# Gathering rows with repeated indices: the first index lists worked out in groups, and five direct batches instead of three

One core of one Trainium2 chip. The metric is the device time of one execution in us, the median of several; a profiled execution gives a trace beside it (its "span" is some 2 us shorter than the device time).

## The reference

```python
# x: (32, 512, 1024) float32, indices: (32, 128) int in 0..511, a fixed random draw
for b in range(32):
    result[b] = x[b, indices[b]]          # (128, 1024) float32
```

A batch writes 128 rows of 4096 B. Its 128 indices repeat: the draw has 109 to 120 distinct ones per batch.

## The kernel before

It reads a repeated row once. For a *direct* batch it gathers all 128 rows and stores them. For a *sparse* batch, VectorE and TensorE first make a list of the distinct indices (with places that spread them evenly over the partitions); GpSimd gathers these rows into one of eight ring buffers, with the unused places out of bounds and so skipped; a matmul with a 0/1 matrix `s` spreads them to the 128 output rows; ScalarE copies these out of PSUM and a store follows. The index work of a sparse batch, three steps in the order of the program (`# ...` and `...` mark cuts; the lines that allocate tiles are left out):

```python
HEAD, RING, FAR, AHEAD = 3, 8, 1024, 9        # HEAD direct batches
pe, dve = InOrder(tc), InOrder(tc)            # what goes through these keeps its program order
# ...
for b in range(HEAD):
    gather(blocks[b], first[...] if b == 0 else idxT[:, b:b + 1], b)
    store(b)
# ...
def step0(b):      # cnt: how many earlier places hold the same index
    pe(mm, bc[:], lhsT=ident[:, col(b)].to_broadcast([N, N]), rhs=vf[:], ...)
    dve(v.scalar_tensor_tensor, out=junk[:], in0=bc[:], scalar=idxF[:, col(b)], in1=below[:], ...,
        accum_out=cnt[:, col(b)])
    dve(... lead16 = (cnt == 0)); dve(... lead = (cnt == 0))
def step1(b):      # nth: which distinct index it is; slot: where it goes
    pe(mm, sm[:, 0:1], lhsT=above[:], rhs=lead16[:, col(b)], ...)
    dve(... nth = sm); dve(... nth ^= shift); dve(... slot = nth)
    dve(v.tensor_scalar, out=pack[:], in0=turn[:], scalar1=slot[:, col(b)], scalar2=lead[:, col(b)], ...)
def step2(b):      # at: the list for the gather; s: the spreading matrix
    pe(mm, sm[:, 0:1], lhsT=pack[:], rhs=near[:, col(b)], ...)
    dve(... at = sm + FAR); dve(... atF = sm + FAR)
    dve(v.tensor_scalar, out=s[:], in0=bc[:], scalar1=atF[:, col(b)], ...)
# ...
for t in range(HEAD, HEAD + AHEAD + 2):       # eleven rounds ahead of any spread
    steps(t)                                  # step0(t), step2(t - 2), step1(t - 1)
    if t - 2 < HEAD + RING:
        fetch(t - 2)                          # gather into a ring buffer
for b in range(HEAD, B):
    spread_rows(b)                            # matmuls ps, copies, store
    fetch(b + RING)
    steps(b + AHEAD + 2)
```

## Time and profile before

| | before |
|---|---|
| time, us | 92.3 (92.2 to 92.9) |
| span of the profiled run, us | 90.1 |
| moved by DMA, MB | 31.99 |
| DMA rate on the plateau, GB/s | 418 |
| sparse gathers ahead of the first spread | 8, one in 1.83 us |
| first spread (start; end of its four matmuls), us | 20.7; 24.4 |

The page cuts the span into 40 slices and gives for each what the DMA engines moved. The useful reading is the *loss*: for a slice of width w and rate r it is (1 - r/418) x w. Added to the bytes over 418 GB/s, the losses give the span; that is so by construction, since the slices together hold all the bytes. The prediction shows the lines themselves.

### The profile page before, as it was taken

The page shows a single profiled execution, that of the slowest core. Times are in us where ns is not written, and L with a number is a line of the kernel's source. Part 1 is how long each engine was busy: PE and PEld are TensorE (multiplying, and loading weights), DVE is VectorE, ACT ScalarE, POOL GpSimd, SP SyncE. Part 2 cuts the span into 40 slices and gives each one's busy share as a digit, 9 for nine tenths or more (in the row PEclk, how much of TensorE's full clock was granted, in tenths as well). Part 3 has the DMA queues.
Part 4 walks back from the last instruction along what each step waited for, and adds up shares of the span by engine and source line. Part 5 has one row for each costly group of instructions (what it writes and reads, how often), then busy time and mean ns, then how long its engine had stood idle before and what let it go on. Part 6 is the DMA issues. An engine that isn't in the chain of part 4 may idle for free.

```text
span 90.1 us, 1046 instructions
## 1 busy us (share of the span) xinstructions
PE 63.1 (70%) x204; PEld 25.6 (28%) x204; DVE 51.3 (57%) x329; ACT 42.9 (48%) x67; POOL 33.7 (37%) x46
## 2 busy tenths in 40 slices
PE   0123232228999999999999999999999988882000
PEld 0110010004434343433434343433444333330000
DVE  2689899988097979787887979797200000000000
ACT  6999300000465555656565655556676755443000
POOL 7764665453054545444444545454440000000000
PEclk9999999999999999999999999999999999999955
DMA  0089999999659999999999999999999999999960
GB/s 2 13 253 324 333 260 393 407 415 411 256 207 249 396 387 420 409 416 416 420 420 415 411 416 418 424 415 420 409 424 418 415 424 413 424 418 418 424 280 7
DMA packets 9415, 31.99 MB, mean 355 GB/s; under 512 B 1590, under 2 KB 1622, under 8 KB 9409
## 3 DMA queue, kind: packets, MB, share of 16 engines
q1 hardware_dynamic: 4800, 16.81, 46.2%
q0 software_dynamic: 4608, 15.12, 44.6%
q14 instruction: 6, 0.04, 0.1%
q8 instruction: 1, 0.02, 0.1%
HBM read 16.81 MB, written 16.78 MB: 373 GB/s over the span
## 4 chain that ended last, share of the span: by engine, by line
DVE 36%; PE 31%; DMA 17%; issue 4%; POOL 1%; ACT 1%; SPq 0%; POOLq 0%; DVEq 0%
PE ps L24 27%; DMA u<-in_x_dram,at 15%; DVE junk L24 7%; DVE s L24 7%; DVE pack L24 6%; DVE nth L24 5%; DVE lead L24 5%; DVE slot L24 3%; PE pos L24 2%; DMA vals<-in_indices_dram 2%; DVE atF L24 1%; DVE at L24 1%; POOL u L110 1%; PE rk L24 1%; ACT block L196 1%
## 5 line engine op out<-in xcount | busy, mean ns | idle before, releaser
L24 PE MATMUL ps<-u,s 128*128 128x512 f32 x116 | 57.1, 625 | 1.5 <-DMA u<-in_x_dram,at 1.5
L196 ACT COPY block<-ps 128x512 f32<-128x512 f32 x58 | 34.0, 586 | 38.5 <-PE ps L24 38.0
L110 POOL DMA_INDIRECT u<-in_x_dram,at x29 | 28.9, 997 | 31.4 <-PE rk L24 13.4
L24 PEld LDWEIGHTS ps<-u,s 128*128 128x128 f32 x116 | 20.5, 194 | 21.2 <-issue 13.2
L24 DVE SCALAR_TENSOR_TENSOR junk<-bc,idxF,below 128x128 f16<-128x128 f32 x29 | 10.1, 349 | 4.5 <-PE rk L24 4.5
L24 PE MATMUL bc<-vf,ident 128*128 128x128 f16 x29 | 6.8, 241 | 6.5 <-DVE s L24 6.5
L24 DVE TENSOR_SCALAR s<-bc,atF 128x128 f32<-128x128 f32 x29 | 10.2, 351 | 1.0
L24 PEld LDWEIGHTS <-pack 128*128 128x128 f16 x29 | 2.9, 100 | 25.1 <-DVE pack L24 24.4
L24 DVE TENSOR_SCALAR pack<-turn,slot,lead 128x128 f16<-128x128 f16 x29 | 9.1, 315 | 1.1
L24 PE MATMUL pos<-near,pack 128*128 128x1 f16 x29 | 5.2, 178 | 6.4 <-DVE pack L24 5.4
L188 ACT COPY u<-zero 128x1024 f32<-128x1024 f32 x8 | 7.7, 1040 | 0.0
L24 DVE TENSOR_SCALAR lead<-cnt 128x1 f16<-128x1 f32 (+1 forms) x58 | 6.2, 150 | 1.0
L24 PE MATMUL rk<-lead,above 128*128 128x1 f16 x29 | 4.8, 164 | 0.8 <-DVE lead L24 0.8
L24 DVE TENSOR_TENSOR nth<-nth,shift 128x1 int32<-128x1 int32 x29 | 4.6, 159 | 1.1
L24 DVE CAST slot<-nth 128x1 f32<-128x1 int32 x29 | 4.5, 154 | 1.0
L24 DVE TENSOR_SCALAR at<-pos 128x1 int32<-128x1 f32 x29 | 4.3, 149 | 0.8 <-PE pos L24 0.5
L24 PEld LDWEIGHTS <-ident 128*128 128x128 f16 x29 | 2.9, 103 | 5.6 <-issue 5.6
L24 DVE TENSOR_SCALAR atF<-pos 128x1 f32<-128x1 f32 x29 | 4.3, 149 | 0.0
L24 DVE CAST nth<-rk 128x1 int32<-128x1 f32 x29 | 4.3, 148 | 0.0
L24 PEld LDWEIGHTS <-above 128*128 128x128 f16 x29 | 3.1, 107 | 0.0
L21 PE MATMUL pos<-ident,vf 128*128 128x32 f16 x1 | 0.2, 209 | 3.2 <-DVE vf L24 3.2
L24 DVE DVE_READ_ACCUMULATOR junk<-bc,idxF,below 128x1 f32 x29 | 2.4, 83 | 0.0
(21 smaller groups left out, 8.3 us busy)
## 6 DMA issues: line engine op xcount, KB each, us to landing
out_dram<-block SPq DMA_DIRECT2D x32, 512.0 KB, 9.2
u<-in_x_dram,at POOLq DMA_INDIRECT x29, 8.9
vals<-in_indices_dram SPq DMA_DIRECT2D x1, 32.0 KB, 1.7
block<-in_x_dram,idxT POOLq DMA_INDIRECT x2, 6.1
first<-in_indices_dram SPq DMA_DIRECT2D x1, 1.0 KB, 1.8
block<-in_x_dram,first POOLq DMA_INDIRECT x1, 4.5
```

The source lines that it names most:

```text
L21: self.last = do(*args, **kw)
L24: self.last = do(*args, **kw)
L110: nc.gpsimd.indirect_dma_start(out=dst[:], out_offset=None, in_=xf[:], in_offset=bass.IndirectOffsetOnAxis(ap=at, axis=0), element_offset= ...
L188: nc.scalar.copy(out=u[:], in_=zero[:].to_broadcast([N, D]))
L196: nc.scalar.copy(out=blocks[b][:, w], in_=ps[:])
```

## The change

It wants the gathers out sooner and the first spread earlier. The first nine sparse batches are worked in groups of 2, 4 and 3: the narrow instructions (one column a batch) are done once for a group, and the scheduler may order the groups' instructions freely. Two more batches become direct, so that GpSimd has gathers to issue meanwhile. The rest of the batches go the old way. `...` marks cuts again, and lines that allocate tiles are left out.

```diff
-    HEAD, RING, FAR, AHEAD = 3, 8, 1024, 9
+    HEAD, RING, FAR = 5, 8, 1024
 ...
-        if not HEAD <= b < B:            # in step0, step1 and step2
+        if not grouped <= b < B:
 ...
+    def group(g0, g1):
+        n, w = g1 - g0, slice(g0, g1)
+        bc = pbc.tile([N, 4, N], F32, name="bc")
+        for b in range(g0, g1):
+            mm(bc[:, b - g0], ...)
+        for b in range(g0, g1):
+            v.scalar_tensor_tensor(out=junk[:], in0=bc[:, b - g0], ..., accum_out=cnt[:, col(b)])
+        for t in (lead16, lead):
+            v.tensor_scalar(out=t[:, w], in0=cnt[:, w], ...)
+        mm(rk[:, :n], lhsT=above[:], rhs=lead16[:, w], ...)
+        v.tensor_copy(out=nth[:, w], in_=rk[:, :n])
+        v.tensor_tensor(out=nth[:, w], in0=nth[:, w], in1=shift[:, w], op=ALU.bitwise_xor)
+        v.tensor_copy(out=slot[:, w], in_=nth[:, w])
+        for b in range(g0, g1):
+            v.tensor_scalar(out=pack[:], in0=turn[:], scalar1=slot[:, col(b)], scalar2=lead[:, col(b)], ...)
+            pe.last = mm(pos[:, b - g0:b - g0 + 1], lhsT=pack[:], rhs=near[:, col(b)], ...)
+        for t in (at, atF):
+            v.tensor_scalar(out=t[:, w], in0=pos[:, :n], ...)
+        for b in range(g0, g1):
+            dve.last = v.tensor_scalar(out=s[:], in0=bc[:, b - g0], scalar1=atF[:, col(b)], ...)
 ...
-    for t in range(HEAD, HEAD + AHEAD + 2):
-        steps(t)
-        if t - 2 < HEAD + RING:
-            fetch(t - 2)
+    bounds = (HEAD, HEAD + 2, HEAD + 6, HEAD + 9)
+    grouped = bounds[-1]
+    for g0, g1 in zip(bounds, bounds[1:]):
+        group(g0, g1)
+        for b in range(g0, g1):
+            if b < HEAD + RING:
+                fetch(b)
+    steps(grouped)
+    steps(grouped + 1)
     for b in range(HEAD, B):
         spread_rows(b)
         fetch(b + RING)
-        steps(b + AHEAD + 2)
+        steps(b + grouped - HEAD + 2)
```

More of the change, by code (lines that the diff above doesn't have):

```diff
@@ L133, in step0 @@
     def step0(b):
-        if not HEAD <= b < B:
+        if not grouped <= b < B:
             return
-        bcs[b] = bc = pbc.tile([N, N], F32, name="bc")
-        pe(mm, bc[:], lhsT=ident[:, col(b)].to_broadcast([N, N]), rhs=vf[:], start=True, stop=True)
+        bcs[b] = bc = pbc.tile([N, 4, N], F32, name="bc")[:, 0]
+        pe(mm, bc, lhsT=ident[:, col(b)].to_broadcast([N, N]), rhs=vf[:], start=True, stop=True)
         junk = junkp.tile([N, N], F16, name="junk")
-        dve(v.scalar_tensor_tensor, out=junk[:], in0=bc[:], scalar=idxF[:, col(b)], in1=below[:],
+        dve(v.scalar_tensor_tensor, out=junk[:], in0=bc, scalar=idxF[:, col(b)], in1=below[:],
             op0=ALU.is_equal, op1=ALU.mult, accum_out=cnt[:, col(b)])
@@ L147, in step1 @@
     def step1(b):
-        if not HEAD <= b < B:
+        if not grouped <= b < B:
             return
@@ L162, in step2 @@
     def step2(b):
-        if not HEAD <= b < B:
+        if not grouped <= b < B:
             return
@@ L172, in step2 @@
         spread[b] = s = pick.tile([N, N], F32, name=f"s{b}")
-        dve(v.tensor_scalar, out=s[:], in0=bcs[b][:], scalar1=atF[:, col(b)], scalar2=None,
+        dve(v.tensor_scalar, out=s[:], in0=bcs[b], scalar1=atF[:, col(b)], scalar2=None,
             op0=ALU.is_equal)
@@ L178, in fetch @@
             gather(held[(b - HEAD) % RING], at[:, col(b)], b, bounds_check=S - 1, oob_is_err=False)
+    def group(g0, g1):
+        n, w = g1 - g0, slice(g0, g1)
+        bc = pbc.tile([N, 4, N], F32, name="bc")
+        for b in range(g0, g1):
+            mm(bc[:, b - g0], lhsT=ident[:, col(b)].to_broadcast([N, N]), rhs=vf[:], start=True, stop=True)
+        for b in range(g0, g1):
+            junk = junkp.tile([N, N], F16, name="junk")
+            v.scalar_tensor_tensor(out=junk[:], in0=bc[:, b - g0], scalar=idxF[:, col(b)], in1=below[:],
+                                   op0=ALU.is_equal, op1=ALU.mult, accum_out=cnt[:, col(b)])
+        for t in (lead16, lead):
+            v.tensor_scalar(out=t[:, w], in0=cnt[:, w], scalar1=0.0, scalar2=None, op0=ALU.is_equal)
+        rk = psm.tile([N, B], F32, name="rk")
+        mm(rk[:, :n], lhsT=above[:], rhs=lead16[:, w], start=True, stop=True)
+        v.tensor_copy(out=nth[:, w], in_=rk[:, :n])
+        v.tensor_tensor(out=nth[:, w], in0=nth[:, w], in1=shift[:, w], op=ALU.bitwise_xor)
+        v.tensor_copy(out=slot[:, w], in_=nth[:, w])
+        pos = psm.tile([N, B], F32, name="pos")
+        for b in range(g0, g1):
+            pack = junkp.tile([N, N], F16, name="pack")
+            v.tensor_scalar(out=pack[:], in0=turn[:], scalar1=slot[:, col(b)],
+                            scalar2=lead[:, col(b)], op0=ALU.is_equal, op1=ALU.mult)
+            pe.last = mm(pos[:, b - g0:b - g0 + 1], lhsT=pack[:], rhs=near[:, col(b)], start=True, stop=True)
+        for t in (at, atF):
+            v.tensor_scalar(out=t[:, w], in0=pos[:, :n], scalar1=float(FAR), scalar2=None, op0=ALU.add)
+        for b in range(g0, g1):
+            spread[b] = s = pick.tile([N, N], F32, name=f"s{b}")
+            dve.last = v.tensor_scalar(out=s[:], in0=bc[:, b - g0], scalar1=atF[:, col(b)], scalar2=None,
+                                       op0=ALU.is_equal)
     def steps(t):
```

## The prediction

> **What bounds the kernel now.** I read the page's 40 slices first, because the kernel moves 32 MB and computes little. A slice is 90.1/40 = 2.25 us; the first line is the busy share of the DMA engines in tenths, the second what they moved.
>
> ```profile
> DMA  0089999999659999999999999999999999999960
> GB/s 2 13 253 324 333 260 393 407 415 411 256 207 249 396 387 420 409 416 416 420 420 415 411 416 418 424 415 420 409 424 418 415 424 413 424 418 418 424 280 7
> DMA packets 9415, 31.99 MB, mean 355 GB/s; under 512 B 1590, under 2 KB 1622, under 8 KB 9409
> ```
>
> From slice 16 to slice 38 the rate is flat, mean 418 GB/s. That plateau is the floor: 31.99 MB / 418 GB/s = 76.5 us. The span is 90.1, so 13.5 us were lost against the plateau, and a slice's loss is (1 - rate/418) x 2.25 us:
> - slices 1 to 3, before a stream exists: 2.24 + 2.18 + 0.89 = 5.3 us
> - slices 4 to 10 (324, 333, 260, then about 400): 2.05 us
> - slices 11 to 15, the hole (256, 207, 249, 396, 387): 3.2 us
> - the last two, emptying: 2.95 us
>
> So nothing done beside the plateau can matter, except its bytes; the hole and the slope ahead of it can. The table by stages says which engine is busy there (columns: stretch, its length, then busy us of each engine, TensorE clock, DMA share, GB/s):
>
> ```profile
> 0.00:7.00 7.00, 0.95 (x8) 0.53 (x8) 4.18 (x30) 6.25 (x7) 4.78 (x17) 1.00 0.32 94
> 7.00:22.00 15.00, 5.01 (x26) 2.00 (x26) 13.53 (x90) 2.69 (x3) 7.98 (x8) 1.00 1.00 364
> 22.00:29.00 7.00, 6.89 (x21) 2.66 (x20) 4.12 (x26) 3.30 (x6) 2.13 (x3) 1.00 0.73 243
> ```
>
> From 7 to 22 us VectorE (third busy figure) is 90% busy, and the transfers get eight gathers. Next the gathers themselves, in the timeline of GpSimd (start, duration):
>
> ```profile
> 5.43 0.94 POOL L110 DMA_INDIRECT block<-in_x_dram,idxT  x1 [0.30 <-issue]
> 7.26 1.00 POOL L110 DMA_INDIRECT u<-in_x_dram,at  x1 [0.89 <-DVE nth L24]
> 9.08 1.00 POOL L110 DMA_INDIRECT u<-in_x_dram,at  x1 [0.81 <-DVE nth L24]
> ...
> 20.04 1.00 POOL L110 DMA_INDIRECT u<-in_x_dram,at  x1 [0.83 <-DVE nth L24]
> 24.69 1.00 POOL L110 DMA_INDIRECT u<-in_x_dram,at  x1 [3.65 <-PE rk L24]
> ```
>
> Direct gathers (the first lines) come 1.25 us apart; sparse ones come every 1.83 us, held by VectorE's index work, and after the eighth there is none for 4.65 us. Why 1.83 is in VectorE's timeline, one period of it:
>
> ```profile
> 8.16 0.14 DVE L24 TENSOR_SCALAR at<-pos 128x1 int32<-128x1 f32 x1
> 8.22 0.15 DVE L24 TENSOR_SCALAR atF<-pos 128x1 f32<-128x1 f32 x1
> 8.40 0.35 DVE L24 TENSOR_SCALAR s<-bc,atF 128x128 f32<-128x128 f32 x1
> 8.67 0.15 DVE L24 CAST nth<-rk 128x1 int32<-128x1 f32 x1
> 8.85 0.16 DVE L24 TENSOR_TENSOR nth<-nth,shift 128x1 int32<-128x1 int32 x1
> 9.05 0.15 DVE L24 CAST slot<-nth 128x1 f32<-128x1 int32 x1
> 9.24 0.31 DVE L24 TENSOR_SCALAR pack<-turn,slot,lead 128x128 f16<-128x128 f16 x1
> 9.47 0.34 DVE L24 SCALAR_TENSOR_TENSOR junk<-bc,idxF,below 128x128 f16<-128x128 f32 x1
> ```
>
> Read the starts, not the durations: `at` to `atF` is 0.06 us, but an instruction that uses the result ahead of it comes 0.18 to 0.20 later (`nth`, `slot`, `pack`). Last, why the hole: in the order of the program eleven rounds of index work stand ahead of the first spread matmul on TensorE, and that one is also slow.
>
> ```profile
> 20.66 3.76 PE L24 MATMUL ps<-u,s 128*128 128x512 f32 x4
> 24.41 1.10 PE L24 MATMUL ps<-u,s 128*128 128x512 f32 x2
> ```
>
> Four of them take 3.76 us here and about 1.96 later. Until they end at 24.4 no ring buffer comes free and no new block can be stored: the three direct stores are done, the eight gathers drain, and the DMA engines stand empty.
>
> **What the Trainium skill says.** "DMA: Bandwidth & Descriptors", section "Where 436 GB/s comes from": the fabric allows 435 GB/s, but the HBM side, about 358, should bind. The trace agrees with the first and not the second: it holds 418 for 50 us, reads and writes of HBM together. I take 418. The same page, section "Queues, rings and completion order": each DMA engine takes turns between the queues that have work. I use this for reads and stores each getting half, some 209 GB/s; the page of before fits (median 8.9 us from issue to landing for a sparse gather, 9.2 for a store) but does not prove it. "VectorE: DVE Perf Modes", section "Two Vector instructions with no wait between them": a next instruction that is not held starts earlier, before the one ahead is finished. The trace agrees: 0.06 against 0.18 us. "SBUF — State Buffer", section "SBUF: two separate sides": VectorE in a two-port mode can lock GpSimd out while it writes a gather's descriptors. Here gathers take 0.94 to 1.00 us beside a 90% busy VectorE, so little of it shows; it is a rival below.
>
> **The change part by part.**
> 1. *Two more direct batches.* They read all 128 rows. The fixed draw has 115 and 111 distinct indices in batches 3 and 4, so 13 + 17 = 30 rows x 4096 B = 0.123 MB more, 0.29 us of plateau. In return, direct gathers need no index work: after those at 2.77, 4.18 and 5.43 two more follow at about 6.68 and 7.93. Five direct stores (2.6 MB) instead of three then wait on the store side.
> 2. *Grouped index work.* Ahead, a batch costs ten VectorE instructions and 1.83 us. In a group of n it costs four wide ones each (`junk` with its accumulator read some 0.34 from start to start, `pack` 0.23, `s` 0.27: 0.84 us) and seven narrow ones for all n. In free order the scheduler has put other groups' `junk` between dependent narrow ones, as the built program's order shows, so I count 0.13 us for a narrow one: 9 x 0.84 + 21 x 0.13 = 10.3 us, from 3.9 to about 14.5. Ahead it was eleven rounds to 20.2.
>    Is GpSimd ever kept waiting? The first group's `at` stands after five wide `junk` for three groups, two `pack` and small ones; summed with these distances it ends at about 7.8, later than the 6.48 of before. But then GpSimd is still at direct gathers until 8.9, so the first sparse one starts at about 9.2. The second group's `at` ends at about 10.7, the third's at about 13.4; gathers 1.3 us apart want them at 11.8 and 17. So all thirteen gathers go out 1.25 to 1.3 us apart, the last at about 18.5.
> 3. *The first spread comes earlier.* On TensorE only `bc` of two batches and one `rk` stand ahead of it now, ready at about 15. It then waits for its gather. At half the rate (209 GB/s from 7.3 us, with some 0.8 MB read before), five direct gathers and one sparse one, 3.09 MB, are there at about 18.3; the slow first four matmuls end at about 22, a little earlier than 24.4.
>    What fills the DMA engines until then? Stores until about 18.5 (2.6 MB at 209 from 7.3 is 12.5 us, held a little by landings), and from there reads alone: by 18.5 about 3.1 of 6.36 MB have been read, the other 3.2 MB last 7.7 us at 418, to 26. New stores come from about 22.5. No hole.
>
> The sum against before: the slope of 2.05 us gives back about 1.5 (slice 4 stays partly short), the hole of 3.2 about 3.0, the bytes cost 0.3: 4.2 us. Start and end stay. After, TensorE's loop of about 2.06 us a batch stays under the DMA's, (0.467 + 0.524 MB)/418 = 2.37 us, so VectorE and TensorE do not bind there. 92.3 - 4.2 = 88.1 us.
>
> **The rivals.**
> - *Reading ahead only moves the hole.* The ring still has eight buffers; if the first spread ended at 26 or later, it would run dry again. For it: the four slow matmuls, and the first group's `at` being later. Against: 3.5 us of margin above. It would give back 1 to 2 us: 89 to 90.
> - *VectorE's dense run slows GpSimd* to, say, 1.8 us a gather. Then the last goes out at 22; but five direct gathers give the reads a backlog that halves at 209 GB/s cannot use up by then, so it costs under 1 us: 88.5 to 89.
> - *The hole was only an idle queue that the later plateau makes up*, since the backlog of stores at the end (last gather landed at 79.5, stores on until 88) hides when things were read. That would make it no gain plus 0.3, 92.6. Against: bytes moved at a flat ceiling cannot be made up later; every us of an empty stretch lengthens the span.
> - *A better case*: slice 3 also fills, and the end shortens: 87.2.
>
> **Range and chances.** The floor argument leaves little room: 87.0 to 90.0 holds the first two rivals and the better case. 2% faster is 90.5; only the third rival, or a group order that stalls GpSimd, misses it. Faster 0.9, same 0.09, slower 0.01.
>
> **What would show each step.** Direct gathers 1.25 us apart up to 7.9 and sparse ones from about 9.2, at 1.3 us, none held by VectorE: step 1 and 2. The slices from 4 on at 390 or more and no slice under 380 up to the last two: step 3. First spread between 17 and 19.5 with its four matmuls near 3.8 us. Plateau still 418, 32.1 MB in all. I am wrong if a hole stands anywhere between 10 and 35 us, if the plateau itself changes, or if the sparse gathers stay near 1.8 us apart.

## The result, and the profile after

| | before | after |
|---|---|---|
| time, us (median; range) | 92.28; 92.20 to 92.94 | 89.27; 88.88 to 89.99 |
| ratio to before (95% interval) | | 0.967 (0.959 to 0.975) |
| span of the profiled run, us | 90.1 | 87.5 |

A ratio is the mean time of one kernel's runs over that of the other's runs of the same rounds, so it is not quite the ratio of the medians quoted beside it. Executions over 1.5% slower than the fastest of the same kernel are left out of the means. A median is that of all runs of a kernel; in fill_2mb, columns_head3, groups_head3_b and first_of_one it takes in one run that counts as slow, in the kernel before of the third group two.

It is 3.0 us faster (3.7 and 3.5 in two repeats below); 4.2 were forecast. First the slices of the changed kernel (2.19 us each), with the DMA engines' busy share above and GB/s below:

```profile
DMA  0088999999999999999999999999999999999960
GB/s 0 15 223 200 257 352 403 419 419 419 419 416 418 419 421 419 418 418 418 419 414 418 418 412 419 418 418 419 418 419 419 418 419 419 419 419 419 419 251 6
DMA packets 9413, 32.11 MB, mean 367 GB/s; under 512 B 1559, under 2 KB 1591, under 8 KB 9408
```

The plateau is 418 as before, 32.11 MB is what was forecast, and there is no hole: from slice 8 to slice 38 no slice is under 412. But slices 3 to 6 (223, 200, 257, 352) are no better than those of before. The "busy" of 0.8 to 0.9 above them is no sign of work: 200 GB/s are moved there. The table by stages, with the columns of the one in the prediction:

```profile
7.00:22.00 15.00, 3.32 (x16) 1.86 (x17) 7.54 (x47) 2.69 (x3) 9.87 (x10) 1.00 0.97 359
22.00:29.00 7.00, 6.89 (x23) 2.82 (x22) 4.99 (x34) 3.51 (x6) 2.66 (x3) 1.00 1.03 421
```

From 7 to 22 us VectorE's load is nearly halved (7.5 us for 13.5) and yet the transfers get 359 GB/s, for 364 before; from 22 to 29 us they get 421 for 243. That is the whole gain. The gathers of the changed kernel, in GpSimd's timeline (the first line is a direct one, the last is the first that reuses a ring buffer):

```profile
8.44 0.94 POOL L110 DMA_INDIRECT block<-in_x_dram,idxT  x1 [0.30 <-issue]
9.68 1.00 POOL L110 DMA_INDIRECT u<-in_x_dram,at  x1 [0.30 <-issue]
10.99 1.00 POOL L110 DMA_INDIRECT u<-in_x_dram,at  x1 [0.30 <-issue]
...
18.80 1.00 POOL L110 DMA_INDIRECT u<-in_x_dram,at  x1 [0.30 <-issue]
24.19 1.00 POOL L110 DMA_INDIRECT u<-in_x_dram,at  x1 [4.40 <-PE rk L24]
```

From the second (4.68) to the thirteenth the gathers go out 1.25 to 1.3 us apart and no sparse one waits for its index list. GpSimd still has nothing to issue for 4.4 us before 24.19, as before. The difference is that the engines still have work queued during this time: slices 10 to 13 (19.7 to 28.4 us) are at 416 to 419. The first spread on TensorE is hardly earlier:

```profile
20.44 3.48 PE L24 MATMUL ps<-u,s 128*128 128x512 f32 x4
23.87 1.96 PE L24 MATMUL ps<-u,s 128*128 128x512 f32 x4
```

And VectorE's timeline in one part of the groups shows what "once for a group" buys: wide instructions that don't need each other follow closely (four `pack` take 0.97 us together, one alone 0.31; four `s` take 1.13), and one narrow instruction serves three or four batches (128x3, 128x4).

```profile
9.15 0.97 DVE L200 TENSOR_SCALAR pack<-turn,slot,lead 128x128 f16<-128x128 f16 x4
10.05 0.15 DVE L194 CAST nth<-rk 128x3 int32<-128x3 f32 x1
10.41 0.16 DVE L204 TENSOR_SCALAR at<-pos 128x4 int32<-128x4 f32 x1 [0.21 <-PE pos L202]
10.49 0.15 DVE L204 TENSOR_SCALAR atF<-pos 128x4 f32<-128x4 f32 x1
10.56 0.15 DVE L195 TENSOR_TENSOR nth<-nth,shift 128x3 int32<-128x3 int32 x1
10.68 1.13 DVE L207 TENSOR_SCALAR s<-bc,atF 128x128 f32<-128x128 f32 x4
```

Where the time went, as losses against 418 GB/s, worked out from the slices of each profile (slices of before are 2.25 us, those of the others 2.15 to 2.24). "Floor" is the bytes over 418. Slices 18 to 38 lose 0.1 or less unless the text says so. The rows under the line are the experiments' profiles:

| kernel | floor | slices 1-3 | slices 4-9 | slices 10-17 | last two | span |
|---|---|---|---|---|---|---|
| before | 76.5 | 5.3 | 2.0 | 3.3 | 3.0 | 90.1 |
| after | 76.8 | 5.3 | 2.4 | 0.0 | 3.0 | 87.5 |
| — | | | | | | |
| again (the changed kernel) | 76.8 | 5.2 | 1.9 | 0.0 | 3.1 | 86.9 |
| after_b (the changed kernel) | 76.8 | 5.2 | 2.0 | 0.0 | 2.6 | 86.6 |
| head5_only | 76.8 | 5.2 | 2.1 | 0.9 | 2.7 | 87.7 |
| groups_head3 | 76.5 | 5.2 | 1.6 | 0.0 | 2.9 | 86.2 |
| groups_head3_b | 76.5 | 5.2 | 2.0 | 0.0 | 2.3 | 86.0 |
| groups_in_order | 76.5 | 5.3 | 2.2 | 0.6 | 2.6 | 87.2 |
| fill_2mb | 81.8 | 3.1 | 1.3 | 0.0 | 3.2 | 89.5 |

Two things stand out. The hole is worth 3.3 us, and every kernel of the table with groups in free order has none of it. The opening (slices 1 to 9) costs 6.8 to 7.7 us in all of them but fill_2mb (4.4), and the same kernel differs in it by 0.6 us from run to run (after 7.7, again 7.1).

### The profile page after: what moved, and what is told of

It reads as the page before. It is cut to its first block, busy times and chain, and to the rows that moved or that the text cites. A ratio compares the mean times of both kernels' runs of the same rounds, so it can differ in the third digit from the quotient of the medians.

```text
span 87.5 us, 931 instructions
## 1 busy us (share of the span) xinstructions
PE 58.3 (67%) x184; PEld 23.8 (27%) x184; DVE 41.8 (48%) x265; ACT 40.5 (46%) x63; POOL 33.6 (38%) x46
## 2 busy tenths in 40 slices
DMA packets 9413, 32.11 MB, mean 367 GB/s; under 512 B 1559, under 2 KB 1591, under 8 KB 9408
## 4 chain that ended last, share of the span: by engine, by line
PE 29%; DVE 29%; DMA 22%; issue 5%; another core or an unknown queue 4%; POOL 1%; ACT 1%; SPq 0%; POOLq 0%; DVEq 0%
PE ps L24 25%; DMA u<-in_x_dram,at 19%; DVE junk L24 5%; DVE s L24 3%; DVE pack L24 3%; DVE s L207 3%; DMA vals<-in_indices_dram 3%; DVE junk L188 3%; DVE lead L24 2%; DVE nth L24 2%; PE pos L24 2%; DVE slot L24 2%; DVE pack L200 1%; DVE atF L204 1%
## 5 line engine op out<-in xcount | busy, mean ns | idle before, releaser
L24 PE MATMUL ps<-u,s 128*128 128x512 f32 x108 | 53.9, 626 | 3.6 <-DMA u<-in_x_dram,at 3.6
L226 ACT COPY block<-ps 128x512 f32<-128x512 f32 x54 | 31.6, 585 | 39.4 <-PE ps L24 31.1
L110 POOL DMA_INDIRECT u<-in_x_dram,at x27 | 26.9, 997 | 26.2 <-PE rk L24 13.0
L24 PEld LDWEIGHTS ps<-u,s 128*128 128x128 f32 x108 | 18.8, 194 | 29.1 <-issue 16.0
L24 PE MATMUL rk<-lead,above 128*128 128x1 f16 x18 | 2.9, 163 | 5.2 <-DVE junk L24 5.2
L24 DVE TENSOR_SCALAR lead<-cnt 128x1 f16<-128x1 f32 (+1 forms) x36 | 3.9, 150 | 4.6 <-remote 4.1
L110 POOL DMA_INDIRECT block<-in_x_dram,idxT x4 | 3.8, 946 | 1.7 <-issue 0.9
L24 PE MATMUL bc<-vf,ident 128*128 128x128 f16 x18 | 3.9, 227 | 0.0
L24 DVE TENSOR_TENSOR nth<-nth,shift 128x1 int32<-128x1 int32 x18 | 2.9, 159 | 0.6
L24 DVE CAST slot<-nth 128x1 f32<-128x1 int32 x18 | 2.8, 154 | 0.6
```

The costliest lines, as they stand in the source:

```text
L24: self.last = do(*args, **kw)
L110: nc.gpsimd.indirect_dma_start(out=dst[:], out_offset=None, in_=xf[:], in_offset=bass.IndirectOffsetOnAxis(ap=at, axis=0), element_offset= ...
L226: nc.scalar.copy(out=blocks[b][:, w], in_=ps[:])
```

## The experiments

Theory: the span is bytes over 418 GB/s, plus what is lost while the DMA engines' queues are empty. The hole is the time between the queues running dry and the end of the first spread, which frees the first ring buffer and gives the first new store. What queues more work ahead of that moment, or brings it forward, closes the hole. (As worded this does not cover all of what came: see the opening under fill_2mb, and the dip of head5_only.) Rivals: only one of the two parts does it; it is the free order that does it. A second question was the opening, where the prediction missed: is it slow because queues are nearly empty, or because of what is read there?

Twelve runs were made in three groups, each group against the kernel before on the same chip (92.9, 92.3 and 92.7 us there). The second group (groups_head4, groups_in_order, fill_2mb, columns_head3) has no run of the changed kernel or of groups_head3 in it and was made on another chip than the other two, so there the ratios to before are what compares.

### again and after_b: the changed kernel twice more

No edit.

> The changed kernel itself, once more, as the control of this group. Expected 0.967 of before, about 89.3 us. Its profile tells what repeats: if VectorE's stretches of 2.0 and 1.7 us with no releaser (12 to 14 and 17 to 19 us of the profile after) are a property of the program they are there again at the same instructions; if they are chance they move. The opening slices (223, 200, 257 and 352 GB/s) should again be well under 418.

> The changed kernel again, as the control of this group. 0.960 to 0.967 of before so far; the loss against 418 GB/s after slice 9 should be zero again, and that of slices 1 to 9 between 7.1 and 7.7 us.

Measured: 89.23 us, ratio 0.960 (0.953 to 0.966), and 89.22 us, ratio 0.962 (0.957 to 0.967). No loss after slice 9. The opening is slow again; in again it reads 236, 260, 332, 371, 345 GB/s in slices 3 to 7.

VectorE's long stretches without a releaser repeat. "remote" in the brackets means that the profile found nothing on this core that ended the wait. In the profile after:

```profile
18.99 0.21 DVE L24 TENSOR_SCALAR lead<-cnt 128x1 f16<-128x1 f32 x2 [1.73 <-remote]
21.82 0.21 DVE L24 TENSOR_SCALAR lead<-cnt 128x1 f16<-128x1 f32 x2 [2.34 <-remote]
```

and in that of again:

```profile
18.45 0.22 DVE L24 TENSOR_SCALAR lead<-cnt 128x1 f16<-128x1 f32 x2 [1.73 <-remote]
21.24 0.21 DVE L24 TENSOR_SCALAR lead<-cnt 128x1 f16<-128x1 f32 x2 [2.31 <-remote]
```

The second stands at the same instruction with the same length in after_b and one_region too (2.32 and 2.35 us), so it belongs to the program and not to chance. The first does not: in these two runs it is 1.20 us, and ended by `junk`. Nor does the stretch of 2.0 us that the expectation named: in again the same `pack` waits 1.25 us, ended by `slot`. In groups_head3 neither of the two is there. What they are, I could not settle. A lock of GpSimd's against VectorE is not it, at least for the second: in again the last gather ahead of it ends at 19.37 and the next starts at 23.23. They cost no time here, since no slice after the ninth lost anything. The first spread of again starts at 19.2; in one_region below, where TensorE was ready by 17.9, it waited for its gather until 19.3.

### head5_only: the direct batches alone

```diff
 # on the kernel before
-    HEAD, RING, FAR, AHEAD = 3, 8, 1024, 9
+    HEAD, RING, FAR, AHEAD = 5, 8, 1024, 9
```

> The kernel before with HEAD 5 instead of 3 and nothing else: index work by single batches in program order. Theory A (the hole is closed by a backlog of reads, and two more direct batches make enough of it): sparse gathers go out from 9.7 us to about 20.6, reads last until about 28, the first spread ends near 25, so no hole: within 0.5 us of the changed kernel, about 89.3. Rival B (the grouped index work closes the hole, by letting the gathers out at 1.3 instead of 1.83 us and the spread start sooner): a hole of some 1.5 to 2.5 us stays, about 91 us.

Measured: 89.54 us, ratio 0.961 (0.954 to 0.968), beside 0.960 of the changed kernel in the same group. Its slices:

```profile
GB/s 0 15 241 295 286 319 375 420 418 418 420 418 417 398 394 321 392 402 413 417 417 420 405 418 417 418 418 418 417 418 420 420 422 418 420 418 422 420 316 13
```

Here the index work is all as before (the first spread starts at 22.8, two us *later* than before), and still the hole has shrunk from 3.3 to 0.9 us; what is left are the 394, 321 and 392 about 33 us. Theory A holds within its 0.5 us; it expected no hole, and a small one is there. A backlog of reads and stores does most of the work, without any faster index work. The dip that is left comes 6 us after the first spread ended (26.5), so it is not the gap that the theory words; neither are the smaller ones of groups_in_order and ring6 below, which also come after the first spread. What they come from was not tested.

### groups_head3 and groups_head3_b: the groups alone

```diff
 # on the changed kernel
-    HEAD, RING, FAR = 5, 8, 1024
+    HEAD, RING, FAR = 3, 8, 1024
```

> The changed kernel with HEAD 3 instead of 5: groups of 2, 4 and 3 in free order, three direct batches. Theory A (either part alone gives the DMA engines enough to do): eleven gathers 1.3 us apart, last at about 17, and the first spread at 15 to 20.5 us, ending 3.5 us later; queued reads and stores (6.9 MB) last to about 24: hole of at most 1 us, less by 0.3 us for the rows saved: 89 to 90 us. Rival B2 (the five direct batches close the hole, the groups do nothing): 91.5 to 92.3, as before.

> Three direct batches with groups in free order, again, beside the changed kernel with more rounds. If it is truly the better one, it is 0.3 to 0.8 us under after_b: 0.29 us for 30 rows that aren't read, the rest from an opening that loses less (6.8 against 7.1 to 7.7 us). If the two are the same, the difference of the first group of runs (0.955 and 0.960) was scatter.

Measured: 88.56 us, ratio 0.955 (0.947 to 0.962), and 88.99 us, ratio 0.960 (0.955 to 0.966). The slices of groups_head3:

```profile
GB/s 0 15 228 317 350 289 407 414 422 418 414 418 424 418 420 414 422 416 412 411 416 420 414 418 422 420 418 411 418 422 424 414 414 420 424 424 411 420 272 6
```

No hole at all: the first spread starts at 15.0 and ends at 18.8. So the groups alone close the hole fully, and beside them the two more direct batches win nothing. The median is under the changed kernel's both times (by 0.7 and 0.2 us), but the intervals overlap. 0.29 us is what the 30 rows not read are worth at 418 GB/s; that it is truly better is not shown.

### groups_head4: four direct batches

`HEAD = 4` in the changed kernel.

> The changed kernel with four direct batches instead of five or three. If the hole is closed by the groups alone, a direct batch costs its extra rows (13 to 17 of 4096 B, 0.13 to 0.17 us) and whatever it does to the opening: between the changed kernel (0.960 of before in the last group) and three direct batches (0.955), so about 0.957. If four is an optimum, because it fills the gap on GpSimd that three leave (5.48 to 7.92 us), it is under 0.953.

Measured: 89.16 us, ratio 0.964 (0.959 to 0.969), where 0.957 was expected. No optimum at four. Between three and five the number of direct batches makes no difference that these runs can tell.

### groups_in_order: groups, but in program order

```diff
 # on groups_head3, in group(): every instruction through pe or dve
-            mm(bc[:, b - g0], ...)
+            pe(mm, bc[:, b - g0], ...)
-            v.scalar_tensor_tensor(out=junk[:], ...)
+            dve(v.scalar_tensor_tensor, out=junk[:], ...)
 ...
```

> Three direct batches, groups of 2, 4 and 3, but every instruction of the groups in program order on TensorE and VectorE instead of free. If the closed hole comes from the fewer instructions and the earlier first spread, and not from the order: index work of nine batches ends some 3 us later than in groups_head3, at about 15, the first spread still starts before 18, no hole, and the time is within 0.4 us of groups_head3. If the free order is what counts (VectorE waiting for TensorE three times a group), sparse gathers fall back to some 1.8 us apart or more, a hole shows and the time is 90 to 91.5 us.

Measured: 88.97 us, ratio 0.965 (0.960 to 0.969).

```profile
GB/s 0 15 231 336 359 265 295 413 419 413 417 417 368 372 412 412 421 415 412 413 419 419 412 419 419 415 419 417 415 419 417 419 419 419 417 419 421 421 325 13
```

The first spread starts at 17.2 and two slices dip to 368 and 372, a loss of 0.6 of the 3.3 us. So grouping gives most of it and the free order the rest in the profile; in the time the order is not told apart from scatter (0.965 against 0.955 and 0.960 in other groups, with intervals that overlap).

### ring6: less room to read ahead

```diff
 # on groups_head3
-    HEAD, RING, FAR = 3, 8, 1024
+    HEAD, RING, FAR = 3, 6, 1024
```

> groups_head3 with six ring buffers instead of eight. Reading ahead stops after nine gathers, the last at about 14.5 us. Queued bytes are then 5.9 MB (9 gathers and 3 stores) and last to about 21; the first spread starts at about 15 and ends near 18.8, so a buffer is free and a store is queued before that: no hole, the same time within 0.4 us, if the theory is right that the hole is the time between queues running dry and the end of the first spread. If it is the number of buffers that closes the hole, one of 1 us or more shows between 17 and 24 us.

Measured: 90.59 us, ratio 0.978 (0.974 to 0.983), against 88.99 of groups_head3_b in the same group: 1.6 us slower, where at most 0.4 were expected.

```profile
GB/s 0 15 231 233 331 281 376 406 417 415 354 402 402 413 408 417 417 417 408 409 419 422 419 419 419 421 419 415 419 417 417 419 419 419 421 421 422 376 274 6
```

The last gather ahead of the first free buffer goes out at 14.95, the next at 20.1 (the first spread waits for its gather until 16.0), and the rate falls to 354 and 402. I had left no allowance for the slow opening, which delays the landing. The two profiled runs differ by 2.0 us of span: the slices from 10 on explain 0.8 of it, slices 4 to 9 another 0.5 and the last two 0.6, and these two terms scatter as much between repeats. So the run fits neither expectation: a hole is there, but of less than 1 us. That a shorter ring brings some of it back, although the first spread ends as early as 19.8, says that an early spread alone doesn't close it; my figure for the margin was wrong.

### one_region: the opening, what is read

```diff
 # on the changed kernel, in gather(): wrong result on purpose (relative error 0.50)
-            element_offset=b * S * D, **kw)
+            element_offset=(b * S * D if kw else 0), **kw)     # direct batches all read batch 0
```

> Wrong result on purpose: the changed kernel with its five direct gathers all reading from the 2 MB of batch 0, with the same count and the same issue times. Theory C (the slow opening is the first touch of each new 2 MB of HBM): from the second gather on the opening slices come up to about 400 GB/s and the time falls by 1 us or more. Rival D (a gather at an almost empty queue exposes the latency of its first rows, whatever they are, because GpSimd issues one in 1.25 us and the engines need 1.25 us for it): the opening stays at 200 to 350 GB/s and the time within 0.4 us of the changed kernel.

Measured: 88.98 us, ratio 0.956 (0.950 to 0.963), beside 89.23 us of again.

```profile
GB/s 0 15 237 205 355 378 331 414 421 419 419 419 417 416 417 416 421 417 421 419 414 417 421 417 419 416 412 416 417 414 421 417 421 421 421 419 421 417 248 6
```

The opening stays at 205 to 378 and the time within 0.3 us. The first touch of each new 2 MB is not why it is slow.

### fill_2mb: the opening, is there room?

```diff
 # on the changed kernel, after the two index loads
+    dense = const.tile([N, 4, D], F32, name="dense")
+    for c in range(4):
+        nc.sync.dma_start(out=dense[:, c], in_=x[B - 1, c * N:(c + 1) * N])    # nobody reads it
```

> The changed kernel with 2.1 MB more of plain loads, which nothing uses, put on the store queue right after the indices: rows of the last batch into a buffer of its own. At the plateau these are 2.10 MB / 418 = 5.0 us. Rival D (the DMA engines are underfed in the opening: GpSimd's gathers alone leave them waiting for the first rows of each) says the opening has room: slices 1 to 6 come up to some 400 GB/s and the time rises by 1 to 2.5 us only. If instead the opening is slow for a reason of the memory or the engines, whatever is queued, the rate there stays under 350 and the time rises by 4 to 5 us.

Measured: 91.37 us, ratio 0.989 (0.985 to 0.994): 2.1 us over the changed kernel's median in the other groups (by the ratios 2.0 to 2.7), where the plateau would take 5.0 for these bytes.

```profile
GB/s 1 283 395 403 383 318 322 412 423 419 415 421 421 417 415 423 419 412 425 415 415 406 417 419 417 419 419 417 421 414 419 423 414 421 423 414 425 404 227 7
```

With plain loads queued, slices 3 to 5 go from 223, 200 and 257 to 395, 403 and 383. So the DMA engines could do more at this time; the opening has room, and about 3 us of it can be had, by traffic that doesn't wait for indices. This kernel has no such traffic: taking one sparse gather away saves only 0.467 MB / 418 = 1.1 us, less than the 2.1 that loading a whole batch costs here.

That looks like rival D, but the trace by queues doesn't fit it (q1 carries loads and stores, q0 gathers; the figures are packets, MB and busy share). The first pair of lines is fill_2mb from 3.87 us, when GpSimd had issued the first gather, to 7.2: the loads moved alone at 400 GB/s, and the gathers not at all. The second is fill_2mb from 11.5 to 14.5 us: the gathers alone moved 309 GB/s, though at 12 us seven were issued (3.55 MB) and only some 1.4 MB of them had moved. The third is the profile after from 24.5 to 27.5 us, where the gathers alone ran at 417.

```profile
DMA packets 371, 1.33 MB, mean 400 GB/s; under 512 B 46, under 2 KB 46, under 8 KB 371
q1 hardware_dynamic: 371, 1.33, 101.3%
DMA packets 254, 0.93 MB, mean 309 GB/s; under 512 B 29, under 2 KB 29, under 8 KB 253
q0 software_dynamic: 252, 0.91, 100.1%
DMA packets 392, 1.25 MB, mean 417 GB/s; under 512 B 87, under 2 KB 87, under 8 KB 392
q0 software_dynamic: 385, 1.24, 101.6%
```

The profile after says the same without the loads. By 6.88 us GpSimd had issued three gathers (1.57 MB), by 9.38 five (2.62 MB); by 9.38 us 1.09 MB of gathers had moved. Work was waiting, and yet from 4.5 to 9.5 us only 224 GB/s ran. ("Issued" means that GpSimd's instruction had ended; even if an engine saw a gather 2.5 us after that, three were there to be moved at 9.38.)

### columns_head3 and first_of_one: two tries at the opening

columns_head3 is groups_head3 with the index columns of all three direct batches in the first small transfer (`first` is [N, 3], and direct batch b takes its column b). first_of_one is groups_head3 with `bounds = (HEAD, HEAD + 1, HEAD + 5, HEAD + 9)`.

> groups_head3 with the index columns of all three direct batches fetched by the first small transfer, so that direct gathers 2 and 3 don't wait for the table of all indices and its transpose: they should start at about 4.05 and 5.3 instead of 4.22 and 5.48. If the opening is bounded by when the first gathers go out, 0.2 to 0.5 us faster than groups_head3; if the small transfer takes longer for three columns (384 elements instead of 128), gather 1 is later by as much and nothing is won.

> groups_head3 with groups of 1, 4 and 4 instead of 2, 4 and 3. The first sparse index list needs two wide VectorE instructions fewer, so the first sparse gather can start some 0.5 us sooner than 7.92, the second later. If GpSimd's gap between the third gather and the fourth (1.5 us) is what keeps the opening low, it gains 0.2 to 0.4 us; if the opening is low because each gather finds empty queues, nothing within 0.2 us.

Measured: columns_head3 89.58 us, ratio 0.964 (0.958 to 0.970), so nothing won. Its direct gathers start at 2.90, 4.32 and 5.58, none earlier than the 2.81, 4.22 and 5.48 of groups_head3, and its first sparse one at 8.87 instead of 7.92. The expectation had a slip: the first gather takes GpSimd 1.11 us and the next comes 0.30 later, which makes 2.77 + 1.41 = 4.18. In groups_head3 the second gather already starts at that distance (4.22, after 2.81). first_of_one: 89.02 us, ratio 0.957 (0.951 to 0.964), within 0.2 us of groups_head3_b; no gain. Its profile fell in a slow run and is not read here. Both were meant to speed the opening up; neither did, and neither says what slows it.

## Why the prediction was right, and where it was not

*The floor argument: right.* That bytes over 418 GB/s and losses add up to the span is only bookkeeping; what the runs show is that the plateau did not change (416 to 418 in all profiles) and that no other slice paid for the hole. The third rival, that an idle stretch is made up later, is refuted: the hole's 3.3 us are gone, and the time fell by 3.0 to 3.7.

*Bytes: right.* 32.11 MB, 0.29 us.

*The hole: right in size* (3.0 forecast, 3.3 found). But the prediction credited it to the two parts together. The experiments show that they are substitutes: five direct batches alone leave 0.9 of 3.3 us, groups alone none. The two together are no faster than either within what was measured. Step 3 had the order of things right and most of its times too early. Its stores were to last until 18.5 (its own sum, 12.5 us from 7.3, makes 19.8, and the total of 8.2 MB at 418 makes 26.9 where it says 26). In the profile after they lasted until about 24.5, since the first began only at about 10; reads alone then ran at 417 until about 27.5. From 14 to 24 us the halves were as forecast: 2.14 MB of gathers and 2.05 MB of stores. They are no rule, though: in fill_2mb the loads went alone for 3.3 us while issued gathers waited.

*When gathers go out: right.* Sparse ones from 9.68 at 1.3 us (forecast 9.2); index lists of the first and second group complete at 7.9 and 10.6 (forecast 7.8 and 10.7). In the profile after everything from the second gather on is 0.5 us late, because the index table landed later in that run (VectorE began on it at 3.64 us, for 2.98 before); in again gathers 4 and 5 start at 6.73 and 7.98, as forecast. The third group's list came at 15.2 instead of 13.4 for the stretches without a releaser; GpSimd got to it at 17.5, so it cost nothing. (The sentence on VectorE that the prediction takes from "VectorE: DVE Perf Modes" stands in that page's section "The DRAIN you can't avoid", which points to the section named.)

*The first spread: right in direction only.* 20.4 (19.2 and 19.6 in the two repeats) against 18.3 forecast, with four matmuls in 3.5 us (3.8 and 3.7). TensorE was to be ready at about 15 and to wait for its gather. The `bc` are there then (14.8), but the `rk` ahead of the spread comes at 17.8 at the earliest (after_b, one_region), at 19.2 in again and 20.4 in after. Of the kernels with five direct batches and groups, only one_region and fill_2mb name a wait for the gather; in after and again the spread follows right behind `rk`. The rival that reading ahead only moves the hole was wrong here, but the margin of 3.5 us was too generous, as ring6 tells.

*The slope: the term that was mis-sized.* "The slope of 2.05 us gives back about 1.5" was the step. It gave back -0.4 us in the profile after, +0.2 and 0.0 in the repeats; of the signs that the prediction named, 390 GB/s or more from slice 4 on failed with it (200, 257 and 352). The supply came as forecast (524 KB every 1.25 us, which is 419 GB/s) and the rate did not: 200 to 350 GB/s. The prediction shows no sum for its 1.5; it seems to have taken the one for the other. one_region says that it is not which 2 MB is read; fill_2mb says that the engines had room for plain loads. It is not that the gathers find empty queues either: in the profile after 1.57 MB were issued by 6.88 us, and 1.09 MB had moved by 9.38. Nor is it the gathers' own queue as such, which alone moved 417 GB/s from 24.5 to 27.5 us. Why the first gathers run at half the rate of later ones stays open. The sum with this term put right: 3.3 - 0.3 - 0.4 - 0.1 = 2.5 us of span, against 2.6 found. That the time lay in the stated range is in part luck: the range reached up to 90.0 for the rivals about the hole, and what came short was the opening.

## What to carry to other kernels

When a DMA plateau is flat, write the span as bytes over the plateau's rate plus the losses of the other slices: each part of a change then has a ceiling, and a hole closed by one part is not closed again by the next. Try the parts alone before keeping both; here a change of one constant gives nearly all of what the rewrite gives. And don't take the rate at which transfers are issued for the rate at which they run: here the first gathers, issued at 419 GB/s, ran at 200 to 350 with more of them waiting.

## What the Trainium skill lacked or had wrong

- "DMA: Bandwidth & Descriptors", section "Where 436 GB/s comes from": its sentence that the HBM side binds at about 358 GB/s for HBM to SBUF does not hold for this run of one core: gathers and stores together, all to or from HBM, hold 418 GB/s for over 60 us in the profile after. The page itself says in its section "Measured (HBM→SBUF, 128 partitions, SWDGE, issued from GpSimd)" that a core alone reached 425 and that about 358 is what each gets when both cores of a pair stream; so the sentence lacks this condition, and the prediction read it without.
- No page that I found has how fast the first back-to-back gathers of a kernel run. Five gathers of 524 KB, 1.25 us apart, moved 200 to 350 GB/s with more of them issued than moved; plain loads of 2.1 MB in the same slices moved 383 to 403, and later gathers alone 417.
- No page that I found explains VectorE standing still for 2.3 us between an accumulator read and the instruction that uses its result, at the same instruction in four runs; in the timeline of before the gap of the same pair is about 0.03 us (9.74 + 0.08 to 9.85).
